# A two-layer decoder trunk: VectorE makes the low parts of the experts' weights that GpSimd made

## The chip, the cores and the metric

The kernel is one program on one core of a Trainium2 chip. The metric is the device time of one execution in microseconds; the time before is the median of three runs, 2014.54 us. The core's engines each have their own instruction queue and run side by side: TensorE (PE in the profile, with its weight loads shown apart as PEld), VectorE (DVE), ScalarE (ACT), GpSimd (POOL) and SyncE (SP), which here issues the loads of the weights. Each engine takes its instructions strictly in the order in which the program gives them.

## The reference

A sequence of 272 tokens (16 learned ones and 256 of the input) of 1024 channels goes through two layers. The first ends in a dense SwiGLU mixer, the second in a mixture of eight experts, of which each token uses two:

```python
for l in range(DEPTH):
    proj = h @ w_in[l]
    # gated linear recurrence and causal convolution, merged by sigmoid gates
    h = layer_norm(DN_ALPHA * h + mixed @ w_out[l], ln1_g[l], ln1_b[l])
    if l % 2 == 0:
        f = swiglu(h, ffn_w_gate[j], ffn_w_up[j], ffn_w_down[j])
    else:
        f = moe_swiglu(h, moe_router[j], moe_w_gate[j], moe_w_up[j], moe_w_down[j])
    h = layer_norm(DN_ALPHA * h + f, ln2_g[l], ln2_b[l])

def moe_swiglu(x, w_router, w_gate, w_up, w_down):
    # top 2 of 8 by the router's logits, softmax over the two
    for e in range(N_EXPERTS):
        out = out + gates[:, e:e + 1] * swiglu(t, w_gate[e], w_up[e], w_down[e])
```

An expert has 3584 hidden columns, so its gate, up and down matrices are 1024x3584, 1024x3584 and 3584x1024 floats. Everything is float32.

## The kernel before

Products run in a float32 format of shorter significand (float32r). To keep float32 accuracy, each factor is split into a high part (the value rounded to float32r) and a low part (the value less the high part), and a product is made of two or three matmuls. Weights are split on the chip, on the way.

**Pieces.** All weights come in pieces of 128 partitions x 1024 floats (512 KB), in one stream of 916: pieces 0 to 243 belong to the two mixers and the dense part (DENSE = 244), pieces 244 to 915 to the experts, 84 to each. `load_ahead` (L269) issues a piece's load on SP into one of six buffers called `raw` (for a while early in the experts' part into six more). `prep` (L282) gives ScalarE the copy raw -> `whi` (through `Tables.activation`, L116 in the profile) and then one engine the subtraction raw - whi -> `wlo`. If that engine is VectorE, the row stands at L94 of the profile (the helper `Priced`), if it is GpSimd at L218, or at L306 for the few pieces whose low parts are put off. `lo_pool` (L315) says by the piece's number which of the two it is. There are six `whi` and six `wlo` buffers (SPLIT); a raw buffer is free for the next load when both parts of its piece are made, a split buffer when TensorE's last product with it is done.

**The experts' part.** Experts are sorted by how many tokens they have, and are worked on by position. Positions 0, 2 and 3 (up to 128 tokens) come first, one after another, then positions 4, 5 and 6 ("slim", up to 64 tokens, whose two parts share one matmul), with one item of position 1 ("wide", up to 256 tokens) strewn in after each group, and at last position 7 (slim). An item is one of gate, up or down for a group of 512 hidden columns, and takes four pieces (`moe_item`, L1452). A normal piece needs six matmuls of 512 columns, a slim one four, a wide one 24 of 256 columns or 12 of 512. The products with `wlo` are those at L1477, L1482, L1490, L1499 and L1503. After each of its four pieces an item calls `prep(self.used + SPLIT - 1)`, so that the split of a piece is put into the queues five pieces ahead of its use.

**What else stands in VectorE's queue there.** In the order of the program, between the low parts: the product of silu(gate) and up (L1559, L1596, L1549), the low parts of the hidden values (`fs`, `fw`, `tmp`, all L94), sums of a wide position (L1530), and for each finished position its y in two parts (L94 `four`, `ys`), a copy of its one-hot matrix (L1610), which TensorE transposes at L1619, and four sums into the output (L1661).

**What GpSimd has there.** The low parts that `lo_pool` gives it and, in the whole stretch of the experts' products, nothing else.

Of the kernel before, what the change touches and what calls it, by code (L numbers as in the profile page):

```python
# [20 lines left out]
S = 256  # L21
T = NM + S
# [11 lines left out]
# Columns of a unit of weights, slots of a narrow and of a slim position, floats of a piece of weights per partition.  # L34
CW, CAP, SLIM, GR = 256, 128, 64, 1024

# Pieces of weights: raw ones, split ones, those of the dense part, and the range in which some of the raw ones
# come from the pool of halves.
# [4 lines left out]
# The product after which a block's evacuation comes; pieces to be ready after pairs of rows; the order of the  # L43
# parts (of the weights, of x) where several blocks are made at once.
# [4 lines left out]
# Experts by position: the first one is fixed, the others are sorted. Wide items after each group, the items before  # L49
# which a gather begins, the groups by which the last position's down products wait.  # L50
# [6 lines left out]
# Columns at which the engines share the rows of tokens, and products that keep the tensor engine's clock up.  # L57
# [11 lines left out]
class Halves:  # L69
    """A [128, 8, n] tensor kept as two tiles of four blocks."""  # L70
# [9 lines left out]
class Priced:  # L80
    """The vector engine, with an estimate of how long it has been given work for."""
# [17 lines left out]
class Tables:  # L99
    """The scalar engine; the functions are taken from three table sets."""  # L100
# [18 lines left out]
class Trunk:  # L119
# [47 lines left out]
    def warm(self, n):  # L167
        """Products that nothing reads: the tensor engine's clock halves when it is left idle for some microseconds."""
        ps = self.ca((P, P))
        for _ in range(n):  # L170
            self.nc.tensor.matmul(ps, self.ones, self.ones, start=True, stop=True)

    def pause(self):
        """Take no more filling work before the next pump."""
        self.t_dve = max(self.t_dve, self.t_pe)
# [34 lines left out]
    def split_half(self, hi, lo, src):  # L210
        """src / 2 == hi + lo."""
        self.A.activation(hi, src, AF.Copy, scale=0.5)
        self.V.scalar_tensor_tensor(lo, src, 0.5, f32(hi), op0=ALU.mult, op1=ALU.subtract)

    def split(self, hi, lo, src, eng=None):
        """src == hi + lo, each part within the float32r significand."""
        self.A.activation(hi, src, AF.Copy)
        (eng or self.V).tensor_tensor(lo, src, f32(hi), op=ALU.subtract)  # L218

# [1 line left out]
    def plan(self):  # L221
# [3 lines left out]
        def piece(w, a, b, c0):  # L225
            """Up to four blocks of rows of a unit's columns."""
            u.append(w[a:b, c0:c0 + CW].rearrange("(k p) n -> p k n", p=P))
# [54 lines left out]
    def prep(self, upto, late=None):  # L282
        """Split the pieces of weights up to `upto` into their two float32r parts, the low ones later if there
        is a list for that."""
# [30 lines left out]
    def lo_pool(self, i):  # L315
        if i >= DENSE:
            return DENSE + 4 <= i < DENSE + 6 or i % 4 == 1 and i < PIECES - 4
        return i != 1 and i < 93 or 156 <= i < DENSE - 8

    def take(self, n):  # L320
        """The next n pieces; [(high, low)] by block of rows."""
# [6 lines left out]
    def gemm(self, x, lo, n, evac, psums=None, start=True, stop=True, kmap=None, kouter=False, before=None):  # L328
        """Two blocks of columns against the tokens lo .. lo + n; evac(block, its psum) comes while the next
        block is under way."""  # L330
# [25 lines left out]
    def gemm_both(self, x, n, evacs, other, before=None):  # L356
        """Two units against all of n tokens, block of rows by block of rows, as x comes."""
# [34 lines left out]
    def level_bits(self):  # L392
        """The bits in which s and t differ, of t after s."""
# [11 lines left out]
    def level_masks(self):  # L405
        """masks[h][s, t]: t is after s, and h is the highest bit in which they differ; masks[0] has the diagonal,
        and masks[1] has it too."""
# [12 lines left out]
    def params(self):  # L420
        """Per-channel parameters, a channel a partition. Those of the first norm come at once, the others
        when params_late is called."""
# [7 lines left out]
        r = 0  # L430
# [58 lines left out]
    def rstd_col(self, mv, k):  # L489
        """mv[:, 1] holds a variance; returns 1 / sqrt(var + eps)."""  # L490
# [6 lines left out]
    def tok_mean(self, t, k, between=None):  # L497
        """[mean, variance] of the rows of t."""
# [23 lines left out]
    def input_norm(self, first):  # L522
        """The normalised tokens, transposed: returns their two parts and the work that makes a block."""
# [22 lines left out]
        def block(b):  # L546
            """The low part of a block waits until the next block is under way."""
# [17 lines left out]
    def norm_sums(self, s, r, first, eng=None):  # L565
        """Add a block to the sums of r and of r * r over the blocks."""
# [16 lines left out]
    def rstd(self, mu, e2, n):  # L583
        """1 / sqrt(e2 - mu * mu + eps)."""
# [16 lines left out]
    def post_norm(self, r, s, g, b):  # L601
        """h = LN(r) * g + b, in two float32r parts; the sums in s have all blocks but the last."""
# [45 lines left out]
    def residual(self, r, h, i):  # L648
        """r block i = ALPHA * h."""
# [3 lines left out]
    def add_to(self, r, ps, b, s):  # L653
        """A block of products added to r, and its part in the sums."""
# [6 lines left out]
    def conv(self, l, u, ready, s, t0, n, out):  # L661
        """Taps of the pairs of blocks in turn; a pair's result takes its input's place. The input is twice
        the gated value, the taps are halved."""
# [42 lines left out]
    def forget(self, l, j, f, k):  # L706
        """f = lb + (1 - lb) sigmoid(z) and k = (1 - lb) sigmoid(-z); lb is zero in the first layer."""
# [11 lines left out]
    def values(self, i, ps, j):  # L719
        """The value projection of a head, copied out; its transposes come a block later."""  # L720
# [20 lines left out]
    def attention(self, hf, f, k, q):  # L741
        """Attention weights of four heads: att[s, t] = sum_d q[t] f[s + 1] ... f[t] k[s], s <= t.
        A level joins neighbouring runs of h tokens: q has the decay from its run's start, k the decay to its
        run's end, and the last of a run's f is the decay of the whole run. A mask keeps the pairs of tokens
        that a level is for; that of runs of one takes a token with itself along."""
# [7 lines left out]
        def runs(x, w, h, r):  # L753
            """The runs of h tokens on side r of their pairs."""
            return x[:, :, w].rearrange("p a (m r h) -> p a m r h", r=2, h=h)[:, :, :, r, :]

        def products(h, r=1):
            """Of the last few tokens of all heads at once, for the mask to keep each head's with itself."""
# [34 lines left out]
        def join(h):  # L793
            """Runs of h tokens become runs of 2 h."""
# [64 lines left out]
    def heads(self, l, sog, o, t0, n):  # L859
        """o = RMS norm of att^T v per head, times the gate (the norm's gain is in it)."""  # L860
# [194 lines left out]
    def spread_rows(self, *names):  # L1055
        """Rows of parameters, put on all partitions by products."""
# [16 lines left out]
    def router_weights(self):  # L1073
        """LN(r) @ W = rstd * (r @ (g W) - mean * sum(g W)) + sum(b W), sums over d: g W and the two sums."""
# [17 lines left out]
    def residual_tok(self, h, res):  # L1092
        """ALPHA * h of the last 256 tokens, tokens on the partitions."""
# [12 lines left out]
    def out_proj1(self, mx, res):  # L1106
        """r = res + mx @ w_out with tokens on the partitions, LN(r), and the router's logits, which are taken
        from r while the last of it is made."""
# [107 lines left out]
    def rank(self, out, x):  # L1216
        """out[e] = number of j with x[j] > x[e], or x[j] == x[e] and j < e; x and out are [128, n, 8]."""
# [11 lines left out]
    def route(self):  # L1229
        """Top two of the logits per token and the place of a token among its expert's; the experts in the order  # L1230
        of their numbers of tokens, but for FIRST, which is at position 0."""
# [48 lines left out]
    def overflow(self, count):  # L1280
        """A number above zero where some position has more tokens than slots."""
# [8 lines left out]
    def gates(self, lg, sel, sorted_by_count):  # L1290
        """Softmax over the two selected logits, by position: its exponentials, then the rest."""
# [20 lines left out]
    def expert_of(self, p):  # L1312
        """The expert at position p, for the addresses of its weights: in a register, but for position 0."""
# [23 lines left out]
    def moe_seq(positions, wide=(), last=None):  # L1337
        """Groups of 512 hidden columns: gate, up, and down one group later. Position 1, which has the most
        products for its weights, is spread over the positions that have the fewest: wide has the number of
        its items after each group."""  # L1340
# [13 lines left out]
    def one_hot(self, ps, key, width):  # L1354
        """[token, token tile, position, slot]: 1 where the token has that slot of the position's expert."""
# [8 lines left out]
    def gather_slim(self, ps, key, now=False):  # L1364
        """The tokens of positions ps: [d, (part, slot)] of each."""
# [38 lines left out]
    def gather(self, ps, key, width, now=False, first=None):  # L1404
        """The tokens of positions ps, transposed: [d, slot] of each, in both parts."""
# [46 lines left out]
    def moe_item(self, kind, p, g, wide, slim):  # L1452
        """One group of 512 hidden columns: products with four pieces of weights."""
# [66 lines left out]
    def gain(self, p, g, ys):  # L1520
        """Add a group's part of y to what the position has."""
# [352 lines left out]
```

## Time and profile before

| | |
|---|---|
| time, median of 3 runs | 2014.54 us (2013.33 to 2029.12) |
| the profiled execution's own span | 2016.8 us |
| first expert product to last | 928.7 to 1999.0 us of the span |
| busy share of the span | PE 95%, VectorE 78%, ScalarE 62%, GpSimd 46% |
| low parts by VectorE (L94 wlo) | 578 rows, 829.9 us |
| low parts by GpSimd (L218 wlo) | 339 rows, 865.5 us |
| high parts (L116 whi) by ScalarE | 919 rows, 950.4 us |

The profile is of one execution, taken by the hardware. A row's time is from its start to its end on its engine; for VectorE and GpSimd this includes time in which the instruction has begun and can't get on. Ends of matmuls are modelled, so that a PE that is "busy" 95% of the time is not a PE at its peak: what tells of lost time is the idle time of the weight loads (PEld) and who ended it. The profiled execution is 2.3 us longer than the median of the runs.

### The profile page before, as it was taken

To read this page: it belongs to the slowest core of one execution; us is meant where nothing else is said; L and a number is where in the kernel's file an instruction comes from. 1 tells how busy PE (TensorE), PEld (TensorE's weight loads), DVE (VectorE), ACT (ScalarE), POOL (GpSimd) and SP (SyncE) were. 2 spreads that over 40 slices of the span, in tenths; PEclk is the share of its full clock that TensorE was granted. 3 is DMA by queue.
4 is the path that set the end of the run, shared out by engine and by line. 5 is a ranking of instruction groups with operands and counts; after the bars stand their busy time and mean duration, and the time that the engine had idled before them with its cause. 6 is when DMAs were issued, how large, how long until landed. Compare 5 with 4: busy or idle time off the path is not lost. (4 is left out here: it accounts for less than half of the span.)

```text
span 2016.8 us, 33666 instructions
## 1 busy us (share of the span) xinstructions
PE 1911.1 (95%) x12193; PEld 1719.1 (85%) x12193; DVE 1571.7 (78%) x1931; ACT 1256.5 (62%) x1707; POOL 930.5 (46%) x424
## 2 busy tenths in 40 slices
PE   9999998999999998998999999999999999999896
PEld 8999898999999998997778888887888887877664
DVE  7998628755568985378999888878878788788887
ACT  5445454544465444645767787777776766766775
POOL 6776756200078567624444444434443433434343
PEclk9999999999999999998999999999999999999998
DMA  6634344565555343564998999998998888999896
GB/s 199 186 116 136 116 128 135 158 176 166 171 157 166 115 126 115 157 204 156 353 335 299 351 358 350 355 334 304 324 317 311 311 312 304 323 316 316 296 344 221
DMA packets 284182, 485.08 MB, mean 241 GB/s; under 512 B 15042, under 2 KB 139842, under 8 KB 284006
## 3 DMA queue, kind: packets, MB, share of 16 engines
q1 hardware_dynamic: 283654, 481.75, 70.7%
q8 instruction: 97, 1.59, 0.3%
q0 software_dynamic: 320, 1.08, 0.1%
q14 instruction: 79, 0.65, 0.1%
q10 hardware_dynamic: 32, 0.01, 0.0%
HBM read 481.73 MB, written 1.05 MB: 239 GB/s over the span
## 5 line engine op out<-in xcount | busy, mean ns | idle before, releaser
L218 POOL TENSOR_TENSOR wlo<-raw,whi 128x1024 fp32r<-128x1024 f32 (+1 forms) x339 | 865.5, 2562 | 1011.4 <-ACT whi L116 970.4
L116 ACT ACTIVATE whi<-raw 128x1024 fp32r<-128x1024 f32 (+1 forms) x919 | 950.4, 1051 | 292.9 <-DMA raw<-in_moe_w_gate_dram 53.6
L94 DVE TENSOR_TENSOR wlo<-raw,whi 128x1024 fp32r<-128x1024 f32 (+1 forms) x578 | 829.9, 1476 | 192.4 <-ACT whi L116 188.1
L343 PE MATMUL mm<-h_hi,whi 128*128 128x272 f32 (+1 forms) x1280 | 378.5, 296 | 1.0 <-ACT tmp L116 1.0
L345 PE MATMUL mm<-h_hi,wlo 128*128 128x272 f32 (+1 forms) x1280 | 371.4, 290 | 0.0
L344 PE MATMUL mm<-h_lo,whi 128*128 128x272 f32 (+1 forms) x1280 | 370.1, 289 | 0.0
L343 PEld LDWEIGHTS mm<-h_hi,whi 128*128 128x128 f32 x1280 | 244.8, 191 | 2.6 <-ACT tmp L116 1.2
L344 PEld LDWEIGHTS mm<-h_lo,whi 128*128 128x128 f32 x1280 | 244.9, 191 | 0.1
L345 PEld LDWEIGHTS mm<-h_hi,wlo 128*128 128x128 f32 x1280 | 244.4, 191 | 0.0
L94 DVE SCALAR_TENSOR_TENSOR st<-wide,cw,st 128x272 f32<-128x272 f32 (+1 forms) x480 | 194.4, 487 | 0.0
L1490 PE MATMUL mm<-wlo,xg 128*128 128x512 f32 x448 | 180.3, 403 | 6.1 <-DVE wlo L94 3.9
L1489 PE MATMUL mm<-whi,xg 128*128 128x512 f32 x448 | 179.0, 400 | 0.0
L1503 PE MATMUL mm<-wlo,xg 128*128 128x512 f32 x336 | 131.8, 392 | 1.4 <-DVE wlo L94 1.3
L1501 PE MATMUL mm<-whi,xg 128*128 128x512 f32 x336 | 132.4, 394 | 0.0
L1502 PE MATMUL mm<-whi,xg 128*128 128x512 f32 x336 | 131.5, 391 | 0.0
L1497 PE MATMUL mm<-xg,whi 128*128 128x256 f32 x448 | 127.6, 285 | 0.0
L1499 PE MATMUL mm<-xg,wlo 128*128 128x256 f32 x448 | 126.8, 283 | 0.0
L1498 PE MATMUL mm<-xg,whi 128*128 128x256 f32 x448 | 126.7, 283 | 0.0
L1477 PE MATMUL st<-wlo,tmp 128*128 128x512 f32 x224 | 96.2, 429 | 22.8 <-DVE wlo L94 11.5
L1490 PEld LDWEIGHTS mm<-wlo,xg 128*128 128x128 f32 x448 | 86.0, 192 | 32.6 <-DVE wlo L94 11.3
L1489 PEld LDWEIGHTS mm<-whi,xg 128*128 128x128 f32 x448 | 86.2, 192 | 19.1 <-issue 0.8
L1476 PE MATMUL st<-whi,tmp 128*128 128x512 f32 x224 | 91.0, 406 | 1.6 <-DVE tmp L94 1.6
(368 smaller groups left out, 3461.8 us busy)
## 6 DMA issues: line engine op xcount, KB each, us to landing
raw<-in_moe_w_gate_dram SPq DMA_DIRECT2D x224, 512.0 KB, 5.2
raw<-in_moe_w_up_dram SPq DMA_DIRECT2D x224, 512.0 KB, 5.8
raw<-in_moe_w_down_dram SPq DMA_DIRECT2D x224, 512.0 KB, 5.1
raw<-in_w_in_dram SPq DMA_DIRECT2D x128, 512.0 KB, 3.8
raw<-in_ffn_w_gate_dram SPq DMA_DIRECT2D x22, 512.0 KB, 4.0
raw<-in_ffn_w_up_dram SPq DMA_DIRECT2D x22, 512.0 KB, 3.9
raw<-in_ffn_w_down_dram SPq DMA_DIRECT2D x20, 512.0 KB, 3.6
raw<-in_w_conv_out_dram SPq DMA_DIRECT2D x16, 512.0 KB, 3.4
```

The source lines that it names most:

```text
L94: return f(out, *a, **k)
L116: return self.eng.activation(out, in_, func, **k)
L218: (eng or self.V).tensor_tensor(lo, src, f32(hi), op=ALU.subtract)
L343: nc.tensor.matmul(ps[c], w[i][0][:, a], xh, start=first, stop=False)
L344: nc.tensor.matmul(ps[c], w[i][0][:, a], xl, start=False, stop=False)
L345: nc.tensor.matmul(ps[c], w[i][1][:, a], xh, start=False, stop=last)
L1489: nc.tensor.matmul(banks[0], x(2 * h + i), whi, start=first, stop=False)
L1490: nc.tensor.matmul(banks[0], x(2 * h + i), wlo, start=False, stop=last)
L1497: nc.tensor.matmul(dst, whi[:, cc], a, start=first, stop=False, skip_group_check=True)
L1501: nc.tensor.matmul(banks[0], a, whi, start=first, stop=False)
L1502: nc.tensor.matmul(banks[0], b, whi, start=False, stop=False)
L1503: nc.tensor.matmul(banks[0], a, wlo, start=False, stop=last)
```

## The change

`lo_pool` decides for the pieces of the experts. Before, GpSimd makes the low parts of pieces 248 and 249 and of every piece whose number leaves 1 when divided by 4 (the second piece of each item), but for the last four pieces of all. After, it makes those of pieces 248 and 249 alone, and VectorE makes all others. In the numbers 244 to 911, 167 leave 1 when divided by 4; one of them is 249, so 166 subtractions of 128x1024 move from GpSimd to VectorE. The rest of the diff takes comments away.

```diff
     def lo_pool(self, i):
         if i >= DENSE:
-            return DENSE + 4 <= i < DENSE + 6 or i % 4 == 1 and i < PIECES - 4
+            return DENSE + 4 <= i < DENSE + 6
         return i != 1 and i < 93 or 156 <= i < DENSE - 8
```

What PE, ScalarE and SP have in their queues, and in which order, is the same before and after. On VectorE the moved rows come in between the others. In a place where slim and wide items alternate (position 5; the rows at L1661 are the sums of the finished position 4 into the output, `fw` is the low part of a wide item's hidden values):

```order
 L94 TENSOR_TENSOR wlo_16312<-raw_16183,whi_16311 128x1024
 L94 TENSOR_TENSOR fw_16280<-four_16276,fw_16279 128x1024
+L94 TENSOR_TENSOR wlo_16328<-raw_16213,whi_16327 128x1024
 L1661 SCALAR_TENSOR_TENSOR res_9776<-ca_16317,gatep,res_9776 128x512
 L94 TENSOR_TENSOR wlo_16341<-raw_16243,whi_16340 128x1024
 L94 TENSOR_TENSOR wlo_16351<-raw_16266,whi_16350 128x1024
 L94 TENSOR_TENSOR wlo_16361<-raw_16289,whi_16360 128x1024
+L94 TENSOR_TENSOR wlo_16376<-raw_16299,whi_16375 128x1024
 L1661 SCALAR_TENSOR_TENSOR res_9776<-ca_16364,gatep,res_9776 128x512
 L94 TENSOR_TENSOR wlo_16389<-raw_16309,whi_16388 128x1024
```

Where three low parts stood between two other rows there are four, in the order of the pieces. The first piece that moves (245) is split while the output projection of layer 1 still runs (L1150 adds its products to the residual, L1151 takes statistics); on VectorE its row comes behind that of piece 244:

```order
 L1151 BN_STATS st_10100<-res_9775 128x6
 L94 TENSOR_TENSOR wlo_10291<-raw_10043,whi_10290 128x1024
+L94 TENSOR_TENSOR wlo_10297<-raw_10078,whi_10296 128x1024
 L1150 TENSOR_TENSOR res_9776<-mm_10261,res_9776 128x256
 L1151 BN_STATS st_10100<-res_9776 128x6
```

There one more row stands ahead of the addition at L1150. On GpSimd, from the same place on (L306 are pieces 248 and 249, L1185 and L1186 finish the layer norm):

```order
 L218 TENSOR_TENSOR wlo_9918<-raw_9665,whi_9917 128x1024
-L218 TENSOR_TENSOR wlo_10297<-raw_10078,whi_10296 128x1024
 L1185 TENSOR_TENSOR res_9775<-res_9775,four_10096 128x768
 L1186 TENSOR_TENSOR res_9775<-res_9775,four_10098 128x768
...
 L306 TENSOR_TENSOR wlo_10461<-raw_10198,whi_10460 128x1024
 L306 TENSOR_TENSOR wlo_10466<-raw_10204,whi_10465 128x1024
-L218 TENSOR_TENSOR wlo_10661<-raw_10212,whi_10660 128x1024
-L218 TENSOR_TENSOR wlo_10730<-raw_10294,whi_10729 128x1024
```

After the two at L306 GpSimd has no work left until the last layer norm.

## Rows read from the trace of the kernel before

**Rows 1.** Stretches: length; PE, PEld, DVE, ACT, POOL busy (instructions); clock, DMA share, GB/s.

```profile
928.70:1062.00 133.30, 126.70 (x566) 100.70 (x567) 126.77 (x113) 97.64 (x108) 58.00 (x20) 0.99 0.87 312
1062.00:1310.10 248.10, 247.82 (x1150) 205.61 (x1149) 211.59 (x178) 194.16 (x209) 108.42 (x42) 1.00 0.95 342
1310.10:1868.00 557.90, 528.13 (x3040) 456.80 (x3039) 455.50 (x356) 390.17 (x452) 222.83 (x83) 0.98 0.90 316
1868.00:1999.00 131.00, 116.81 (x504) 83.31 (x503) 113.03 (x98) 101.95 (x126) 53.27 (x20) 0.97 0.89 316
```

**Rows 2.** Idle time of PEld, 928.7 to 1310.1: total us, times, longest.

```profile
PEld ca L1566 <- DVE tmp L1559: 7.9, 8, 1.7
PEld mm L1503 <- DVE wlo L94: 3.5, 5, 1.3
```

**Rows 3.** The same, 1310.1 to 1868.

```profile
PEld st L1477 <- DVE wlo L94: 19.8, 23, 2.2
PEld st L1477 <- POOL wlo L218: 13.3, 11, 1.5
PEld ca L1619 <- DVE tmp L1610: 7.1, 2, 4.7
PEld ca L1482 <- DVE wlo L94: 4.2, 4, 2.3
```

**Rows 4.** The same, 1868 to 1999.

```profile
PEld mm L1490 <- DVE wlo L94: 10.3, 17, 1.4
PEld st L1477 <- DVE wlo L94: 5.6, 14, 0.7
PEld st L1477 <- POOL wlo L218: 4.5, 4, 1.7
```

**Rows 5.** Timeline, 1526 to 1537: start, us, count, idle before; POOL, then DVE.

```profile
1524.99 3.25 POOL L218 TENSOR_TENSOR wlo<-raw,whi 128x1024 fp32r<-128x1024 f32 x1 [4.51 <-PE mm L1489]
...
1526.55 7.23 DVE L94 TENSOR_TENSOR wlo<-raw,whi 128x1024 fp32r<-128x1024 f32 x3
...
1529.96 2.74 POOL L218 TENSOR_TENSOR wlo<-raw,whi 128x1024 fp32r<-128x1024 f32 x1 [1.72 <-ACT whi L116]
```

**Rows 6.** 400 to 500: the stretch as in rows 1, and L94's ns min/median/max.

```profile
400.00:500.00 100.00, 100.00 (x795) 100.00 (x795) 54.78 (x69) 45.11 (x69) 0.00 (x0) 1.00 0.59 171
...
L94 DVE TENSOR_TENSOR wlo<-raw,whi x33: 1224/1226/1227, 400.5 to 497.4; 128x1024 fp32r<-128x1024 f32 x33
```

**Rows 7.** Timeline of DVE at 951: three low parts back to back.

```profile
951.10 3.49 DVE L94 TENSOR_TENSOR wlo<-raw,whi 128x1024 fp32r<-128x1024 f32 x3
```

**Rows 8.** Lines L94 and L218, 928.7 to 1999: ns min/median/max.

```profile
L94 DVE TENSOR_TENSOR tmp<-tmp,tmp x28: 424/1559/1742, 1334.8 to 1989.8; 128x256 fp32r<-128x256 f32 x28
...
L94 DVE TENSOR_TENSOR fw<-four,fw x7: 1214/3410/3416, 1365.9 to 1846.3; 128x1024 fp32r<-128x1024 f32 x7
...
L218 POOL TENSOR_TENSOR wlo<-raw,whi x165: 2354/2544/3473, 938.3 to 1988.7; 128x1024 fp32r<-128x1024 f32 x165
```

**Rows 9.** DVE's low parts in the four stretches: busy, mean ns, idle before.

```profile
L94 DVE TENSOR_TENSOR wlo<-raw,whi 128x1024 fp32r<-128x1024 f32 x62 | 109.0, 1808 | 8.7 <-ACT whi L116 8.6
...
L94 DVE TENSOR_TENSOR wlo<-raw,whi 128x1024 fp32r<-128x1024 f32 x126 | 176.8, 1444 | 31.0 <-ACT whi L116 30.1
...
L94 DVE TENSOR_TENSOR wlo<-raw,whi 128x1024 fp32r<-128x1024 f32 x252 | 367.7, 1504 | 83.4 <-ACT whi L116 80.2 <-PE st L1476 1.9 <-PE mm L1499 0.7
...
L94 DVE TENSOR_TENSOR wlo<-raw,whi 128x1024 fp32r<-128x1024 f32 x62 | 87.4, 1456 | 11.1 <-ACT whi L116 11.0
```

**Rows 10.** DVE's timeline at 900, where piece 245's low part comes in.

```profile
900.21 0.42 DVE L1150 TENSOR_TENSOR res<-mm,res 128x256 f32<-128x256 f32 x1 [1.30 <-PE mm L1140]
```

**Rows 11.** Stretches as in rows 1, at the end of a position.

```profile
1685.00:1690.00 5.00, 0.70 (x4) 0.69 (x4) 5.00 (x5) 4.05 (x5) 2.12 (x2) 0.86 0.95 361
1690.00:1695.00 5.00, 5.00 (x14) 3.85 (x13) 5.00 (x4) 2.80 (x5) 2.63 (x1) 0.50 0.46 122
```

**Rows 12.** The stretch of position 3 alone, as in rows 1.

```profile
1185.80:1310.10 124.30, 124.02 (x576) 102.78 (x575) 103.95 (x89) 96.84 (x105) 53.08 (x21) 1.00 0.98 353
```

## The prediction

> **What bounds it now.** I read four views in turn. First the stretches [rows 1]: the experts' products run from 928.7 to 1999.0, 1070.3 of the span's 2016.8 us, and nothing that the change moves lies elsewhere but for one piece. In these stretches PE is busy 95% or nearly all of the time, VectorE 95, 85, 82 and 86%, the loads run at 312 to 342 GB/s. No engine is alone the bound. The fastest stretch for loads has 353 GB/s, at a DMA share of 0.98 [rows 12]; a piece of 0.524 MB then takes 1.485 us, 84 pieces 124.8 us, and position 3 took 124.3. Between 1062 and 1310 the loads and PE's own work are the pace, and nothing that concerns low parts can be won there.
>
> Second, who kept the weight loads waiting, since an idle PEld is lost time here while a busy PE is partly modelled. Up to 1310: 7.9 us on the product that is to be transposed (VectorE, L1559) and 3.5 on low parts [rows 2]. From 1310 to 1868: 37.3 us on low parts, 13.3 of them by GpSimd and 24.0 by VectorE (19.8 + 4.2), and 7.1 on L1610, which stands behind low parts in VectorE's queue [rows 3]. From 1868: 20.4 on low parts [rows 4]. So low parts that come late cost up to 76 us in all (11.4 + 44.4 + 20.4), in which some of the waits only hide another.
>
> Third, why they come late. At 1526 VectorE takes 7.23 us for three low parts, while two of GpSimd's lie across them, 3.25 and 2.74 us long [rows 5]. Where GpSimd does nothing for 100 us, all 33 of VectorE's low parts take 1224 to 1227 ns [rows 6]; in the experts' stretches they take 1444 to 1808 in the mean [rows 9]. Two smaller subtractions show the same: 1559 ns in the median at a least of 424, and 3410 at a least of 1214 [rows 8]. So a subtraction on VectorE that meets one on GpSimd stands until that one is done.
>
> Fourth, the clock. After 5 us in which PE was busy 0.70 us (it waited for L1610), its granted clock is 0.50 for the next 5 us, the lower of its two levels [rows 11].
>
> **The change, step by step.**
>
> *Taken from GpSimd*: 166 subtractions, 165 of them in the four stretches (20, 42, 83 and 20) [rows 1], each 2544 ns in the median [rows 8]. Nothing queues behind them there.
>
> *Given to VectorE*: the same 166. Three in a row take 3.49 us, 1.163 each [rows 7], since their starts overlap a little. 165 x 1.163 = 192 us.
>
> *Taken from VectorE*: what GpSimd adds to it. The low parts it already has take 109.0 + 176.8 + 367.7 + 87.4 = 740.9 us for 502 rows [rows 9]; at 1.163 they would take 583.8, so 157 us go. The two smaller kinds lose about 28 x 1.14 = 32 and 7 x 2.20 = 15 us by their medians [rows 8]; I take 40 for both. Together 197: VectorE's busy time stays where it is (906.9 + 192 - 197 = about 902 us). By stretch, with 1.163 for each low part: position 0, 126.8 - 109.0 + 82 x 1.163 = 113 of 133 us; positions 2 and 3, 211.6 - 176.8 + 168 x 1.163 = 230 of 248; slim and wide, 455.5 - 367.7 + 335 x 1.163 - 34 = 443 of 558; position 7, 113.0 - 87.4 + 82 x 1.163 - 6 = 115 of 131 [rows 1, 9].
>
> A rule weighs the price otherwise. The rows give a price of 197 / 165 = 1.2 us that one subtraction of GpSimd costs VectorE. The Trainium skill, "SBUF — State Buffer", section "Who interferes with whom", says that a VectorE instruction with two SBUF inputs and a GpSimd instruction that reads SBUF exclude each other, and that whoever comes second is blocked for the other's whole length. By that alone one could be charged up to 2.5 us each, 420 us in all; the trace agrees with the blocking, not with that total, since VectorE is idle for 15% of these stretches [rows 1], and an instruction that began first is not held up.
>
> *In the order*: on VectorE three rows become four between the others. The place at 1526 [rows 5] is then 4 x 1.163 = 4.65 us instead of 7.23, and what is queued behind (the sums at L1661, then the next low parts) comes earlier. Where GpSimd did not hit, the same place grows from 3.49 to 4.65, and what is behind comes 1.16 us later; the split is queued five pieces ahead of its use, which covers that where PE takes 1.4 us and more a piece, and does not in a slim run, where PE takes less. The moved low part itself takes 1.2 instead of 2.5 us, but waits for its turn.
>
> *Piece 245*, ahead of L1150: VectorE idles 1.30 us there until PE is done [rows 10], so its 1.16 costs nothing; without that cover, 1.2 us. SP's queue has no new wait: a raw buffer comes free after either part as before.
>
> **The sum**, as time off the stretch:
> - 928.7 to 1310: of 11.4 us of waits [rows 2] I take 5, for VectorE's load in position 0 falls from 127 to 113. Bounds 0 and 11.
> - 1310 to 1868: of 13.3 us on GpSimd's parts 10, since they take half as long; of 24.0 on VectorE's own half, 12; of 7.1 on L1610 a third, 2; and 2 for the clock, half of a 5 us stretch at half speed [rows 11]. 26. Bounds 0 and 47.
> - from 1868: 20.4 us of waits [rows 4], but 84 pieces can't come faster than 124.8 us, and it takes 131.0: 4. Bounds 0 and 6.
> - Positions 2 and 3: VectorE goes from 85 to 93% busy; where its queue then stands full at a bad moment, PE waits. I take 3 us lost, bounds 0 and 12.
>
> 5 + 26 + 4 - 3 = 32 us off 2016.8, 1984.8. That execution is 2.3 us over the median of the runs, so **1983 us** against 2014.54, 1.6% faster. With all waits gone and nothing lost: 64 off, about 1950.
>
> **Rivals.**
>
> *The wait only changes hands.* VectorE is as busy as before, and PE waits for the same engine; ScalarE's high parts come late instead (VectorE idled 8.7 + 31.0 + 83.4 + 11.1 = 134 us ahead of low parts, nearly all for `whi` [rows 9]). For it: the busy sum does not fall. Against it: where VectorE is not idle at all, in position 0, its load does fall by 14 us, and GpSimd's own late parts are gone. Time 2005 to 2017, say 2010.
>
> *Slower by VectorE's waits in order.* Ahead of its low parts VectorE idles 134 / 502 = 0.27 us each, in the mean, for its `whi`. GpSimd took that wait beside VectorE for the pieces that now move; 165 x 0.27 = 44 us more in one queue. It decides if VectorE is the pace, that is if its busy 902 us and idle time together fill the stretch: 1070 + 44 - 5 (busy saved), 39 us slower, 2053. Against it: the idle time is there because VectorE is ahead, and shrinks when it is not.
>
> *Slower because the long rows are not GpSimd's doing.* If VectorE's low parts stay at 1.52 us (740.9 less two small ones, over 500), 665 of them take 1011, and with 166 us of other work VectorE needs 1177 in a stretch of 1070: 107 us slower, 2121. It decides above (1070 - 166) / 665 = 1.36 us a part. The 33 rows at 1.226 [rows 6] speak against it. The Trainium skill's "Perfetto Trace Analysis", section "Optimizing Scalar/DVE Operations", would have work moved off a saturated VectorE, to GpSimd too, and adds that the read port they share may leave no gain; the trace bears out the second half.
>
> **How the numbers follow.** A measurement of this kernel can tell about 1% from no change. The forecast with its neighbours (15 to 60 us off) 0.63; the wait changes hands (within 15 us) 0.24; slower in order 0.10; rows that stay long 0.03. Faster by over 1% means under 1994.4, 20 us off: 0.60 of the first case's 0.63. Within 1%: 0.30, the second case and the edges of the others. Slower: 0.10. For the range I leave out the highest tenth (most of the two slower cases) and the lowest: 1957 to 2018. The likeliest case's own range is 1955 to 2000.
>
> **What would show it.** Right: VectorE's low parts at 1.2 us with hardly any over 1.3; its busy time from 928.7 on near 900 us; `tmp` at 0.42 and `fw` at 1.21; no wait of PEld on GpSimd; less wait on L1619; position 0 below 130 us, positions 2 and 3 as before, slim and wide near 532 us, with loads at 330 GB/s; position 7 at 125 to 128. Wrong: waits of PEld on VectorE's low parts that grow by what GpSimd's lose; positions 2 and 3 longer by 10 us; VectorE's idle time ahead of low parts over 150 us.

## The result, and the profile after

The changed kernel takes 1991.18 us in the median of 4 runs (1983.78 to 1993.68), the kernel before 2018.28 in 4 runs beside it (2013.33 to 2029.12): a ratio of 0.9849, 95% interval 0.9814 to 0.9884, 1.5% faster, or 27.1 us by the medians. The forecast was 1983 us, 1.6% faster, and the range holds the time.

The profiled executions span 2016.8 and 1991.8 us, 25.0 apart. The experts' stretch, from the first expert product to the last, went from 1070.3 to 1038.4 us: 31.9 less. The other 7 us lie ahead of it, where the first expert product came at 935.8 instead of 928.7 us. In the ten later traces of kernels that leave the part ahead alone it came between 930.6 and 935.8, in that of the unchanged kernel before at 931.7 and in that of the changed one at 934.5: mostly scatter of a few us of the part ahead. The two traces of the kernel before lie at the low end, so a delay of some 3 us by the change is not excluded. The stretch is what I compare from here on.

The same four stretches of the changed kernel, with the boundaries at the same items (columns as in [rows 1]):

```profile
935.80:1059.90 124.10, 123.90 (x567) 102.32 (x567) 113.01 (x134) 98.00 (x108) 0.00 (x0) 0.99 0.92 339
1059.90:1307.50 247.60, 247.60 (x1150) 205.63 (x1149) 230.93 (x221) 196.44 (x210) 0.00 (x0) 1.00 0.96 343
1307.50:1846.60 539.10, 521.59 (x3039) 452.71 (x3038) 446.67 (x436) 386.24 (x450) 0.00 (x0) 0.99 0.92 325
1846.60:1974.20 127.60, 115.28 (x505) 85.10 (x503) 113.61 (x118) 100.86 (x126) 0.00 (x0) 0.97 0.91 332
```

VectorE (the third busy figure) executes 909 instructions where it had 745 [rows 1], the new ones being the moved low parts (one of other kinds falls outside the boundaries), and is busy 113.01 + 230.93 + 446.67 + 113.61 = 904.2 us, against 906.9. GpSimd is busy for none of it, against 442.5.

Line 94 from 935.8 to 1974.2, in ns as least/median/most, answers to [rows 8], and the timeline of VectorE at the place of [rows 5]; its columns are start, length, and the count at the end:

```profile
L94 DVE TENSOR_TENSOR wlo<-raw,whi x667: 684/1222/1228, 939.4 to 1972.8; 128x1024 fp32r<-128x1024 f32 x167
L94 DVE TENSOR_TENSOR tmp<-tmp,tmp x28: 424/426/428, 1330.3 to 1965.5; 128x256 fp32r<-128x256 f32 x28
L94 DVE TENSOR_TENSOR fw<-four,fw x7: 1216/1219/1220, 1361.4 to 1828.9; 128x1024 fp32r<-128x1024 f32 x7
```

```profile
1520.89 4.62 DVE L94 TENSOR_TENSOR wlo<-raw,whi 128x1024 fp32r<-128x1024 f32 x4
1525.43 0.74 DVE L1661 SCALAR_TENSOR_TENSOR res<-ca,gatep,res 128x512 f32<-128x512 f32 x1
```

No low part takes over 1228 ns. In the kernel before, the median was 1212 ns as well; 122 of its 500 full low parts took over 1400 ns and brought the mean to 1522. All of these 122 overlap a row of GpSimd, and the 113 that overlap none take 1206 to 1226 ns. `tmp` fell from 1559 to 426 and `fw` from 3410 to 1219 in the median. At the place shown, four low parts stand in 4.62 us where three stood in 7.23.

What PEld waited for, from 1307.5 to 1846.6 and then from 1846.6 to 1974.2 (total us, times, longest), answers to [rows 3] and [rows 4]; ahead of 1307.5 only 0.9 us of waits is left in all, none of it in the lines of [rows 2]. In the second list the five largest of eleven are shown:

```profile
PEld st L1477 <- DVE wlo L94: 16.5, 34, 1.2
PEld ca L1619 <- DVE tmp L1610: 5.9, 2, 3.7
PEld ca L1590 <- ACT tmp L116: 5.2, 8, 1.2
PEld mm L1489 <- ACT whi L116: 4.5, 4, 1.1
PEld ca L1658 <- DVE four L1530: 1.4, 1, 1.4
PEld mm L1490 <- DVE wlo L94: 0.3, 1, 0.3
```

```profile
PEld mm L1490 <- DVE wlo L94: 7.9, 12, 1.7
PEld st L1477 <- DVE wlo L94: 5.9, 12, 1.1
PEld ca L1619 <- DVE tmp L1610: 3.1, 1, 3.1
PEld st L1476 <- ACT whi L116: 3.0, 3, 1.2
PEld mm L1489 <- ACT whi L116: 2.4, 2, 1.5
```

The waits on GpSimd are gone and those on VectorE's low parts did not grow; waits on ScalarE (ACT) have come in.

### The profile page after: what moved, and what is told of

It reads as the page before. It is cut to its first block, busy times and chain, and to the rows that moved or that the text cites. A ratio compares the mean times of both kernels' runs of the same rounds, so it can differ in the third digit from the quotient of the medians.

```text
span 1991.8 us, 33645 instructions
## 1 busy us (share of the span) xinstructions
PE 1900.0 (95%) x12193; PEld 1718.2 (86%) x12193; DVE 1576.9 (79%) x2097; ACT 1253.4 (63%) x1707; POOL 487.7 (24%) x258
## 5 line engine op out<-in xcount | busy, mean ns | idle before, releaser
L94 DVE TENSOR_TENSOR wlo<-raw,whi 128x1024 fp32r<-128x1024 f32 (+1 forms) x744 | 881.9, 1218 | 182.5 <-ACT whi L116 164.4
L218 POOL TENSOR_TENSOR wlo<-raw,whi 128x1024 fp32r<-128x1024 f32 (+1 forms) x173 | 423.0, 2464 | 366.4 <-ACT whi L116 353.0
L94 DVE SCALAR_TENSOR_TENSOR st<-wide,cw,st 128x272 f32<-128x272 f32 (+1 forms) x480 | 194.5, 491 | 0.0
L1497 PE MATMUL mm<-xg,whi 128*128 128x256 f32 x448 | 127.6, 285 | 0.0
```

Of the source, the lines that this page charges most:

```text
L94: return f(out, *a, **k)
L1497: nc.tensor.matmul(dst, whi[:, cc], a, start=first, stop=False, skip_group_check=True)
```

## The experiments

Two things changed at once for the moved pieces, and the time alone can't separate them.

- *Theory A*: GpSimd's subtractions blocked VectorE's, so VectorE's own low parts came late. Taking them away gives VectorE back what the moved work costs it.
- *Theory B*: GpSimd's own low parts came late, since one takes 2.5 us there and 1.2 on VectorE. Blocked or not, PE then waits for every fourth piece.

All edits below are made to the changed kernel. The stages of each run, in us, are in this table, from the first product of a position to that of the next; here the third stage ends with the first product of position 7, some us after the boundary used above.

| kernel | position 0 | positions 2, 3 | slim and wide | position 7 | stretch |
|---|---|---|---|---|---|
| before | 133.3 | 248.1 | 561.8 | 127.2 | 1070.3 |
| before again (`e0_before`) | 134.0 | 247.9 | 555.1 | 127.6 | 1064.5 |
| after | 124.0 | 247.6 | 543.1 | 123.6 | 1038.4 |
| after again (`e10_after`) | 122.3 | 247.6 | 548.2 | 121.7 | 1039.9 |
| `e1_gpsimd_too` | 150.3 | 296.5 | 615.6 | 151.5 | 1214.0 |
| `e2_gpsimd_fills` | 122.3 | 247.6 | 542.7 | 123.0 | 1035.7 |
| `e3_pos0` | 123.8 | 247.8 | 556.4 | 124.6 | 1052.8 |
| `e5_mix` | 134.0 | 250.5 | 545.3 | 126.3 | 1056.1 |
| `e8_later` | 123.6 | 255.1 | 555.7 | 129.6 | 1064.0 |
| `e9_token` | 123.7 | 247.6 | 582.7 | 126.5 | 1080.6 |
| `e6_l1610` | 123.3 | 247.6 | 538.2 | 123.3 | 1032.4 |
| `e11_l1610_again` | 123.4 | 247.6 | 539.1 | 122.9 | 1033.0 |
| `e7_dense` | 122.3 | 247.6 | 542.8 | 123.3 | 1036.0 |

**The two kernels again.** The unchanged kernel before, traced a second time:

> The kernel before, unchanged, for a second trace. The profile after reached the first expert product at 935.8 us, that of before at 928.7, though nothing up to piece 245 differs. If that is scatter between executions, this trace reaches it anywhere between about 925 and 940, and the experts' stretch (928.7 to 1999.0, 1070.3 us) repeats within 5 us. If the change itself delays the part ahead, this trace shows 928 to 930 again.

It took 2015.88 us, with the first expert product at 931.7 us and a stretch of 1064.5, 5.8 less than in the first trace. The unchanged kernel after, once more:

> The kernel after, unchanged, beside the others of this call: 1991, give or take 5.

1987.79 us (1984.54 to 1994.21) against 2022.38 for the kernel before beside it, ratio 0.9826 [0.9805, 0.9847]. The gain repeats. By the means of the two traces of each, position 0 is 10.5 us shorter, positions 2 and 3 0.4, slim and wide 12.8, position 7 4.8; a single stage moves by up to 7 us between two executions of one kernel, so smaller differences of it are not read.

**GpSimd subtracts too, beside VectorE.** VectorE makes all low parts as in the changed kernel, and GpSimd makes those of every fourth piece a second time, into a scratch tile that nobody reads, in three strips of up to 384 columns (the line that makes the tile is left out here).

```
+            if i >= DENSE and i % 4 == 1 and i < PIECES - 4 and not self.lo_pool(i):
+                for a, b in ((0, 384), (384, 768), (768, m)):
+                    self.nc.gpsimd.tensor_tensor(self.scratch[:, :b - a], t[:, a:b], f32(hi[:, a:b]), op=ALU.subtract)
```

> The kernel after, but GpSimd makes the moved low parts too, in three strips of 384, 384 and 256 columns into a scratch that nobody reads. TensorE never waits for GpSimd. Theory A (a subtraction of GpSimd holds up those of VectorE): VectorE's low parts are back at 1.4 us and more, its busy time in the experts' stretch goes from 908 to some 1100 us, more than the stretch of 1039 has, so 2050 us or more. Theory B (the gain came only from GpSimd's low parts being late, 2.5 us instead of 1.2): 1991 us, give or take 8.

2165.11 us (2161.77 to 2176.49), ratio 1.0748 [1.0707, 1.0789]. The experts' stretch as in [rows 1], line 94 and GpSimd's line by their ns, and the largest wait of PEld (its lines are 4 higher than in the changed kernel):

```profile
931.50:2145.40 1213.90, 1070.82 (x5256) 863.29 (x5254) 1153.31 (x907) 783.06 (x895) 801.85 (x495) 0.96 0.82 284
```

```profile
L94 DVE TENSOR_TENSOR wlo<-raw,whi x667: 681/1683/2077, 934.0 to 2144.0; 128x1024 fp32r<-128x1024 f32 x167
L310 POOL TENSOR_TENSOR scratch<-raw,whi x498: 725/1617/3254, 899.1 to 2134.9; 128x384 f32<-128x384 f32 x166
```

```profile
PEld st L1481 <- DVE wlo L94: 68.4, 69, 3.2
```

The same VectorE instructions are busy 1153 us instead of 904, their median goes from 1222 to 1683 ns, and GpSimd's strips, too, grow to about twice their least in the median (1884 against 997 for those of 384 columns, 1607 against 725 for those of 256). Nothing waits for GpSimd's results, so this is blocking by itself: theory A's mechanism is there, and both engines pay. Its size is not that of the kernel before. GpSimd here is busy 802 us against 442.5, and a raw buffer now comes free only when the strips are done too: SP's loads waited for the strips 133 times, 297.7 us in all. The run shows the sign and the cause, not the price.

Rows of VectorE with one operand in PSUM are not longer: L1559 took 683 ns at most in the kernel before, and 680 here (where it is L1563).

**GpSimd is as busy, but reads next to nothing.** In place of the strips, a copy of one column (to start at the same moment) and six fills of the scratch tile, under the same condition.

```
+                self.nc.gpsimd.tensor_copy(self.scratch[:, :1], f32(hi[:, :1]))
+                for _ in range(6):
+                    self.nc.gpsimd.memset(self.scratch, 0.0)
```

> The kernel after, and at each moved piece GpSimd reads one column of the high part and then fills a scratch of 384 columns with zeros six times: about as long busy as with a subtraction, but reading next to nothing. If what holds VectorE up is that both read SBUF (theory A with the reading side), VectorE's low parts stay at 1.22 us and the time at 1991, give or take 8. If any work of GpSimd holds VectorE up, low parts of 1.4 us and 2030 us or more, as in the run with the subtractions. Theory B: 1991.

1991.2 us (1989.55 to 1993.1), ratio 0.9874 [0.9851, 0.9896], as the changed kernel. The same views:

```profile
935.20:1970.90 1035.70, 1008.42 (x5256) 847.50 (x5255) 904.77 (x907) 782.02 (x895) 596.29 (x1155) 0.99 0.93 333
```

```profile
L94 DVE TENSOR_TENSOR wlo<-raw,whi x667: 682/1220/1228, 937.7 to 1969.5; 128x1024 fp32r<-128x1024 f32 x167
```

GpSimd's two kinds of work in this stretch (busy, mean ns):

```profile
L311 POOL MEMSET scratch<- 128x384 f32 x990 | 416.0, 420 | 57.3
L309 POOL COPY scratch<-whi 128x1 f32<-128x1 f32 x165 | 180.3, 1093 | 376.0 <-ACT whi L116 375.4
```

Of the 596 us, 416 are fills, nearly as long as GpSimd was busy in the kernel before (442.5). The rest are the one-column copies, which read and mostly stand: 185 ns at least, 1171 in the median. VectorE does not feel the fills: 904.8 us, median 1220 ns. So it is not GpSimd's activity that holds VectorE up, but its reading of SBUF beside a subtraction that reads two tiles there. The Trainium skill, "SBUF — State Buffer", section "Who interferes with whom", states just this: a VectorE instruction with two SBUF inputs contends with a GpSimd instruction that reads SBUF, and not with one that only writes it. The two traces agree, 1683 against 1220 ns.

**One part of the change alone: position 0.** GpSimd makes every fourth low part again from position 2 on.

```
-            return DENSE + 4 <= i < DENSE + 6
+            return DENSE + 4 <= i < DENSE + 6 or i >= DENSE + 84 and i % 4 == 1 and i < PIECES - 4
```

> Only position 0's low parts move (pieces 245 to 327), the others stay with GpSimd as before. If position 0 gains by VectorE's lower load there (127 to 113 us busy), its stretch is 124 us as in the kernel after, and the rest as before (248, 558, 131): a stretch of 1061 us instead of 1070. If what position 0 gained in the profile after (9 us) was scatter, 133 and 1070.

2006.97 us in a single run, stretch 1052.8: position 0 took 123.8 us as after, the others stood within the scatter of before, position 7 (124.6) nearer to after. Position 0's 10 us are a gain of its own, and it is not given back later.

**One part alone: slim and wide.** VectorE makes all low parts only for the pieces of that stage.

```
-            return DENSE + 4 <= i < DENSE + 6
+            return DENSE + 4 <= i < DENSE + 6 or not DENSE + 252 <= i < DENSE + 588 and i % 4 == 1 and i < PIECES - 4
```

> Only the low parts from piece 496 to 831 move (positions 4 to 6 and the wide one), the others stay with GpSimd as in the kernel before. If what a stretch gains comes from that stretch alone: 134 and 248 us for positions 0 and 2 and 3 as before, 543 in place of 555 to 562 for the slim and wide part, 124 to 127 for position 7; a stretch of 1049 to 1053 in place of 1064 to 1070.

2007.62 us in a single run, stretch 1056.1: that stage took 545.3 us, in the range of after, position 0 134.0 as before. Positions 2 and 3 took 250.5, 2.5 longer than in either kernel, which I can't explain. Within the scatter of single traces the two parts of the change add up: 14.6 and 11.3 us off the mean stretch before, of 28.2 in all.

**VectorE makes them, but late.** Against theory A alone: no GpSimd instruction stands beside VectorE, but each moved low part is issued one piece later in VectorE's order, so that it comes late without GpSimd.

```
+            held, self.held = self.held, []
+            if late is None and DENSE + 6 <= i < PIECES - 4 and i % 4 == 1:
+                self.A.activation(hi[:, :m], t[:, :m], AF.Copy)
+                self.held.append(lambda a=(lo[:, :m], t[:, :m], f32(hi[:, :m])): self.V.tensor_tensor(*a, op=ALU.subtract))
+            elif late is None:
...
+            for f in held:
+                f()
```

> The kernel after, but each moved low part (from piece 253 on) stands one place later in VectorE's queue, behind that of the next piece: it is ready some 3.4 us after its high part, later than GpSimd had it (2.6 in the median of the trace before), and GpSimd does nothing. If a late second piece was worth much by itself (theory B, 13.3 + 7.9 us of TensorE's waits before), most of that comes back: 2005 to 2012 us. If the blocking was nearly all (theory A): 1991 to 1998.

2014.13 us (2008.27 to 2015.43), ratio 0.9967 [0.9952, 0.9982]. Its largest waits of PEld (lines 7 higher):

```profile
PEld st L1484 <- DVE wlo L94: 31.0, 22, 2.3
PEld mm L1497 <- DVE wlo L94: 27.4, 23, 3.1
```

VectorE's low parts still take 1218 ns in the median, and yet nearly all of the gain is gone, more than either theory was given. All of the 63.5 us of waits on low parts are on the held ones. So lateness alone can cost as much as the whole change wins. But it is more lateness than GpSimd's. By the ends of the two parts of a piece in the trace, the held low part ends 4.1 us after its high part in the median; GpSimd's ended 2.6 after it in the kernel before, and VectorE's end 1.26 after it in the changed kernel. Of the loss, 7.5 us lie in positions 2 and 3, where GpSimd's lateness cost nothing before. Position 0 kept its gain (123.6): there lateness costs nothing, and what it won was VectorE's own time.

**A last touch by GpSimd.** A smaller lateness was meant: VectorE makes the moved low part at its place, and GpSimd then makes its first column again, which delays the piece by little and leaves GpSimd hardly busy.

```
+            if late is None and DENSE + 6 <= i < PIECES - 4 and i % 4 == 1:
+                self.nc.gpsimd.tensor_tensor(lo[:, :1], t[:, :1], f32(hi[:, :1]), op=ALU.subtract)
```

> The kernel after, and behind each moved low part (from piece 253 on) GpSimd makes its first column once more, with the same value. TensorE has to wait for that one: the second piece is ready about 2.4 us after its high part, as it was with GpSimd before (2.5), but GpSimd holds VectorE up by one column at most and VectorE's load is that of after. A run with 4.1 us of lateness cost 23 us. Theory A (blocking alone): 1991 to 1995. Theory B (lateness counts too): TensorE's lateness on second pieces goes from 8 back towards 20 us, 2000 to 2008.

2035.86 us (2033.74 to 2037.04), ratio 1.0071 [1.0053, 1.0089]: slower than the kernel before. GpSimd's line by its ns (lines 2 higher), PEld's largest wait, and from the timeline at 1443 one case:

```profile
L308 POOL TENSOR_TENSOR wlo<-raw,whi x165: 186/192/5594, 943.8 to 2004.5; 128x1 fp32r<-128x1 f32 x165
```

```profile
PEld st L1479 <- POOL wlo L308: 44.3, 17, 6.9
```

```profile
1442.96 6.90 DVE L94 TENSOR_TENSOR wlo<-raw,whi 128x1024 fp32r<-128x1024 f32 x6
...
1444.32 5.74 POOL L308 TENSOR_TENSOR wlo<-raw,whi 128x1 fp32r<-128x1 f32 x2 [6.68 <-DVE wlo L94]
...
1449.96 0.80 PE L1479 MATMUL st<-wlo,tmp 128*128 128x512 f32 x1 [6.51 <-POOL wlo L308]
```

Most of the 165 touches took 0.19 us, as meant. But where VectorE has several low parts in a row, the touch stands until the last of them. Here there are six, from 1442.96 to 1449.86; the first is the one that is touched, and the touch stands from 1444.32 until the other five are done. GpSimd's two touches are over at 1450.06, and PE waited 6.5 us for a column. PEld waited for touches 17 times, 44.3 us in all. The stretch is 41 us longer than after, most of it in slim and wide. There PEld's waits are 60.3 us in sum against 33.8 and 35.9 in the two traces of after, and the mean granted clock is 0.96 against 0.99; so the lower clock has a part in the loss. The lateness was not the one meant, neither forecast came true, and what GpSimd's lateness alone was worth is not settled by it.

**The copy at L1610, too.** The wait on L1610 is left in the changed kernel (5.9 + 3.1 us above), since the copy stands behind low parts in VectorE's queue. Here the idle GpSimd makes it.

```
-            self.nc.vector.tensor_copy(t, x[:, :, None, :].to_broadcast([P, 2, 2, SLIM]))
+            self.nc.gpsimd.tensor_copy(t, x[:, :, None, :].to_broadcast([P, 2, 2, SLIM]))
```

> The kernel after, with the copy of the one-hot matrix at L1610 (128x256, one per slim position) made by GpSimd, which has nothing else to do there. After, weight loads still wait 9.0 us for it, as it stands behind low parts and the two halves of y in VectorE's queue. If TensorE has nothing else to wait for there, that goes and with it some of the time at the lower clock: 6 to 12 us off, 1980 to 1985. If the next thing in the queue is late as well: 1988 to 1992.

1983.14 us (1981.29 to 1987.55), ratio 0.9822 [0.979, 0.9854], stretch 1032.4. And again beside the second run of the changed kernel:

> The kernel after with the copy at L1610 on GpSimd once more, on the same chip as the kernel after: if the 6 us that its experts' stretch was shorter (1032 against 1038) are its own, 5 to 9 us under the kernel after; if they were scatter, within 3 us of it.

1984.77 us (1983.84 to 1988.56), ratio 0.9823 [0.9803, 0.9842], against 1987.79 for the changed kernel beside it; stretch 1033.0. PEld's largest waits of the second:

```profile
PEld st L1477 <- DVE wlo L94: 20.7, 41, 1.2
PEld mm L1490 <- DVE wlo L94: 16.0, 23, 1.7
```

No wait on L1619 is left, and low parts cost 36.7 us in place of the changed kernel's 30.8 (22.5 + 8.3 over its stretch). The stretch is 6 to 7 us shorter than after both times. In the medians of the two run side by side it is 3 us, which isn't clear of the scatter. Its medians are the lowest of the kernels run.

**The same for the dense part.** VectorE makes the low parts of pieces 156 to 235 too.

```
-        return i != 1 and i < 93 or 156 <= i < DENSE - 8
+        return i != 1 and i < 93
```

> The kernel after, and VectorE also makes the low parts of pieces 156 to 235 (80 of GpSimd's in the dense mixer and in layer 1). Theory A in another place: 80 subtractions of 2.4 us that no longer hold up VectorE's, against 80 x 1.2 = 96 us more work for it. VectorE is 57% busy from 500 to 600, but 92% and 78% from 600 to 800, and most of its rows there are not of two operands in SBUF. If the bargain holds as in the experts' part: up to 8 us off, 1983. If VectorE fills up in the mixer of layer 1: 5 to 20 us more, 1996 to 2011.

2016.48 us (2014.84 to 2022.25), ratio 0.9991 [0.9975, 1.0006]: the whole gain lost, more than was expected, with an unchanged experts' stretch (1036.0). The first expert product came at 960.3 instead of 935.8. A stretch of it (columns as in [rows 1]), and PE's largest wait between 500 and 960:

```profile
700.00:800.00 100.00, 75.94 (x652) 74.58 (x650) 94.71 (x195) 33.48 (x59) 6.59 (x9) 0.89 0.37 116
```

```profile
PE st L597 <- DVE sums L94: 29.4, 1, 29.4
```

VectorE is busy 94.71 of these 100 us with 195 instructions; in the changed kernel it is busy 87.36 with 146, and no wait of PE from 500 to 960 is over 3.6 us in all. What stands ahead of the sums that came late, and then the same sums in the changed kernel, 63 us earlier:

```profile
780.82 23.59 DVE L94 SCALAR_TENSOR_TENSOR st<-wide,cw,st 128x256 f32<-128x256 f32 x60
804.54 0.43 DVE L94 TENSOR_TENSOR sums<-sums,wide 128x256 f32<-128x256 f32 x1
```

```profile
741.77 0.43 DVE L94 TENSOR_TENSOR sums<-sums,wide 128x256 f32<-128x256 f32 x1
```

So PE waited behind 60 rows of the convolution, not behind low parts. From 450 us to the first expert product VectorE has the same 541 other rows in both kernels, but in another order, which no other edit here brought about. Why the order changed (the kernel puts work aside by an estimate of VectorE's load, which these low parts raise) is argued from the code.

There was blocked time to win back here, too. One kind of row that reads two tiles of SBUF, in the changed kernel and in this one (busy, mean ns):

```profile
L94 DVE TENSOR_TENSOR k<-k,c 128x512 f32<-128x512 f32 x8 | 10.2, 1276 | 1.1 <-PE ca L817 1.1
L94 DVE TENSOR_TENSOR k<-k,c 128x512 f32<-128x512 f32 x8 | 5.9, 739 | 0.0
```

Summed over the 541 rows it is 47.8 us less, for 97.9 us of new low parts. The 80 subtractions of GpSimd had cost VectorE 0.6 us each, half of what they cost in the experts' part, and making them costs 1.22. The run does not tell how much of its loss is this worse bargain and how much the new order.

## Why the prediction was right

**The mechanism, as forecast.** VectorE's long low parts were GpSimd's doing: 1222 ns with 1228 at most, busy 904 us where 902 were forecast with 165 low parts more. By stages 113, 231, 447 and 114, said 113, 230, 443 and 115. The place of [rows 5] takes 4.62 us for four, said 4.65. The two runs with a busy GpSimd (1683 and 1220 ns) show that it takes a GpSimd that reads. The price of 1.2 us of VectorE per GpSimd subtraction holds for the experts' part: 165 more low parts cost it nothing.

**Position 0: said 5 off, 9.2 in the pair and 10.5 by the means.** Under-sized. I counted under half of the 11.4 us of waits in [rows 2] since some waits only hide another. These went altogether, only 0.9 us is left in other lines, and nothing stood behind them. Done alone, it gave the same.

**Positions 2 and 3: said 3 lost, 0.5 gained.** VectorE is busy 93% of the time there as said, and PE had no wait on it; the loss did not come.

**Slim and wide: said 26 off, 18.8 in the pair and 12.8 by the means.** This is the term that was too large. Its own parts were near: waits on low parts fell from 39.2 us (37.3 in [rows 3] and 1.9 in two lines left out there) to 16.8, 22.4 less where 22 were said, and those on L1610 from 7.1 to 5.9 (said 5). The granted clock in the 5 us behind that wait was 0.67 instead of 0.50 [rows 11]:

```profile
1675.00:1680.00 5.00, 4.74 (x15) 3.84 (x16) 5.00 (x7) 3.82 (x5) 0.00 (x0) 0.67 0.86 297
```

What I had not costed are the waits that come next: 5.2 us on ScalarE's copy at L1590, 4.5 on its high parts and 1.4 on L1530, 11.1 in all where the kernel before had 1.4 in other lines. With them, 22.4 + 1.2 - 9.7 = 13.9 us of waits went in the pair, 12.4 in the second traces (48.3 to 35.9). That is the rival "the wait only changes hands", true for some 10 of the 26 us. The prediction named ScalarE's high parts in that rival and put nothing of them into the sum.

The term for the clock, 2 us, was smaller than what the clock does between two executions of one kernel. By the granted clock that the traces record, 20.5 us of this stage were at the lower of the two levels in the first trace of before and 3.4 in the second, 6.8 and 13.7 in those of after. Half of such time is lost to PE, as the lower level is half the higher. With the waits this estimate gives 20.7 us off for the first pair and 7.3 for the second; measured were 18.7 and 6.9. So the pair's 18.8 is in part luck with the clock; about 13 us went by the waits, and by the means of the stage.

**Position 7: said 4, 3.4 in the pair and 4.8 by the means.** It took 127.6 us by the prediction's boundary, near the 124.8 in which its pieces were said to come at best. That the loads were what stopped it is not shown: they came at 332 GB/s there, under the 353 of [rows 12], and PEld still waited 27.9 us, 13.8 of them on low parts. (PE was busy 89% in this stretch before [rows 1], not the 95% or more of the prediction; nothing rests on that.)

**The sum.** Said 32, 31.9 in the pair of profiles; 28.2 by the means of two traces each; 27.1 and 34.6 by the medians of the two comparisons. The terms' errors (4 to 6 too little in position 0, 3.5 in positions 2 and 3, 7 to 13 too much in slim and wide) mostly cancel, so that the total came out better than its parts is luck.

**The causes behind it.** The prediction named both VectorE's blocked parts and GpSimd's late ones, and costed them at 12 and 10 us of slim and wide. By the traces, told apart by piece, PEld's waits on low parts were 22.4 us on the second pieces of the items (GpSimd's, but for the last) and 45.5 on the others before, and 9.3 and 21.4 after. So a third of the 37 us that went was on GpSimd's own pieces and two thirds on VectorE's, and the second traces give the same (21.7 and 44.6, 8.4 and 19.4). The held parts show that a larger lateness alone takes the gain away; no run gave GpSimd's lateness without blocking at its true size, so the split by a run stays open.

**The rivals.** "Slower by VectorE's waits in order" fell: VectorE idled 121.7 us ahead of all its 665 low parts, not 134 + 44:

```profile
L94 DVE TENSOR_TENSOR wlo<-raw,whi 128x1024 fp32r<-128x1024 f32 x665 | 789.3, 1222 | 121.7 <-ACT whi L116 103.6 <-PE mm L1499 0.6 <-PE mm L1490 0.5
```

"The long rows are not GpSimd's doing" fell with the 1222 ns. Its price was too high, too: 1.52 us is the mean length of rows whose starts overlap. By busy time it is 740.9 / 502 = 1.48 us a part, which makes 665 parts 982 us and the kernel some 78 us slower, not 107.

## What to carry to other kernels

The busy time of an engine holds the time in which a neighbour blocked it, so look for a stretch where the neighbour is idle and read the same instruction there: here 1.226 us against means of 1.4 to 1.8, and the work that had been given to GpSimd to relieve VectorE cost VectorE as much as it saved. When a wait is taken away, read who is late next on the engine that waited, not only what the moved work costs its new engine. And work out the bargain anew for each place: in the dense part the same move gave VectorE back half of what it cost, and the kernel's other work came in another order, in which PE waited 29 us.

## What was not expected of the hardware

A GpSimd subtraction of a single column, 0.19 us in the median, stood up to 5.59 us beside VectorE's subtractions back to back. In the case shown, five of them ended while it stood, and four of these had begun after it: it got no turn between two of them. In the kernel before, whose low parts on GpSimd are as long as two of VectorE's, the longest was 3.47 us at a median of 2.54 [rows 8]. And 416 us of GpSimd's fills beside the same VectorE work cost 1 us of busy time at most (904.8 against 904.2).
